# Moving the scale and shift of a normed operand to GpSimd, and re-staging a mixer's input projection

## The chip, the cores and the metric

The kernel runs on one core of a Trainium2 chip. The metric is the device time of one execution in microseconds (us). The core's engines work side by side and wait for one another by semaphores: TensorE (PE, matrix products), VectorE (DVE), ScalarE (ACT), GpSimd (POOL) and SyncE (SP, which issues the transfers). Each runs its own list of instructions in the order in which the program wrote them.

## The reference, cut to what matters

A diffusion backbone of two layers works on 384 tokens: 256 latent ones and 128 of context. Each layer is a feed-forward stage, a mixer and another feed-forward stage, all in fp32.

```python
h = rmsnorm(x, g_norm[l, 0]) * (1.0 + sc1) + sh1
x = x + 0.5 * gt1 * swiglu(h, ffn1_w13[l], ffn1_w2[l])
h = rmsnorm(x, g_norm[l, 1]) * (1.0 + sc2) + sh2
m, k_state, v_state = mixer(h, l, ctx_kv, use_rope)
x = x + gt2 * m
h = rmsnorm(x, g_norm[l, 2]) * (1.0 + sc3) + sh3
x = x + 0.5 * gt3 * swiglu(h, ffn2_w13[l], ffn2_w2[l])
...
# in the mixer
proj = h @ w_in[l]
z, q, k, v, gates = split(proj)
u, zv = split(gelu(z))
a = u * (w_spatial @ rmsnorm(zv, sgu_gain) + b_spatial)      # gating unit, in chunks of 128 tokens
b = differential attention of q, k, v                        # 8 heads, rotary on the latent tokens
m = (sigmoid(g_a) * (a @ w_branch_a) + sigmoid(g_b) * (b @ w_branch_b)) @ w_out
```

`sc`, `sh` and `gt` come from a modulation product of the conditioning vectors, one set for the context tokens and one for the latent ones.

## The kernel before, in words

**Three products for one.** TensorE multiplies in a rounded fp32 format, so every operand is held as two parts: `hi` (a rounded copy, made by ScalarE, L406 for activations and L180 for weights) and `lo` (the rest, a subtraction on VectorE, L409 and L183). Each product is the sum of hi x hi, lo x hi and hi x lo (`mm3`, L232 to L234; L386 to L388 in token-major form). Weights come in chunks of 128 x 1024 (`raw`), loaded by SP ahead of time and split into `whi` and `wlo`, four buffers each, by `split_upto`; the `lo` halves are deferred by a few steps.

**Jobs.** The program is a list of jobs, written out in the order in which TensorE is to do them. A column job (`col_job`) makes one 128 x 384 tile of a result in eight k-steps of three matmuls. A token-major job set (`tokmajor_job`) makes three accumulators of 128 x 512 in four jobs; its operands are swapped, so that tokens lie on the partitions. Both take PSUM buffers `mm` from a ring of four. After its matmuls a job's `evac` is written; the next job follows. Other work is written between jobs: `bg`, a list of functions of which `run_bg` pops one (or two while more than six are left) at the start of each job with a weight chunk, and `mods.put()`, which writes one step of the modulation product (mostly two VectorE passes over a 128 x 1024 chunk, L437; at a piece's end two reductions, L443).

**The lead of a stage.** While the norm of x is not yet known, products start on the operand `u` = x times the scale (unnormed, with the shift in two extra columns, so 386 wide), and the evacuation applies the norm: `normed` copies the two shift columns (L607) and multiplies the PSUM tile by the broadcast norm `rb` (L608), both on VectorE, and ScalarE then applies the function with the shift as bias (L725 in the mixer, L645 in the feed-forward). `lead` takes the first columns this way: three as a group, the others as column jobs. Beside the latter, `make_h` makes the operand `h` proper, eight tiles: POOL multiplies x by `rb` (L564), ScalarE applies scale and shift in two pieces, for the latent and the context tokens (L573), and the tile is split (L406, L409). The tiles pass through `t`, five buffers that the evacuations use as well. A feed-forward stage has eight such columns, the mixer six. Five of the six stages have a lead; the first stage of layer 0 starts in another way.

**The mixer's order.** The lead makes six of the eight tiles of `u` in the reference's sense (tile `m["u"]`, columns u0 to u5). Then come two token-major sets for `zv` (`zv_evac`, L735, L736), with a modulation step after each job; then `push_sgu` puts the gating unit into `bg` (the norm `sgu_norm`; the scales of the token groups 0 and 1; the scale of group 2 with block 0; blocks 1 to 7). Columns u6, u7 (with a modulation step after each), q and k of head 0, and two token-major sets for v follow, then attention with the rest of the columns woven in. A block is six matmul instructions on TensorE (L764) and then VectorE (L768, L771) and a split; its PSUM tile `tp` has one buffer. `zv` and `v` share a slot (`spare("Z", 1)`), so the first v evacuation flushes `bg`. The k evacuation copies k on ScalarE and turns it by the rotary on VectorE (L784 to L787).

Of the kernel before, what the change touches and what calls it, by code (L numbers as in the profile page):

```python
# [11 lines left out]
AF = mybir.ActivationFunctionType  # L12
ALU = mybir.AluOpType
AX = mybir.AxisListType

P = 128
D = 1024
# [16 lines left out]
SH1, SC1, GT1, SH2, SC2, GT2, SH3, SC3, GT3 = range(9)  # L34
TOK = ((1, 0, 256), (0, 256, 384))
# [5 lines left out]
def hybrid_step(  # L41
# [5 lines left out]
    T, V, S, G = nc.tensor, nc.vector, nc.scalar, nc.gpsimd  # L47
# [29 lines left out]
    modT = cp.tile([P, DEPTH, 9, KD, 2], F32, name="modT")  # L77
    amod = cp.tile([P, 3, KD, 2], F32, name="amod")

    x = cp.tile([P, KD, NT], F32, name="x")  # L80
# [84 lines left out]
    def run_later(n=1):  # L165

        for e in later:
            e[0] -= n
        while later and later[0][0] <= 0:
            later.pop(0)[1]()  # L170
# [25 lines left out]
    bg = []  # L196

    def run_bg(n=1):
        for _ in range(n):
            if bg:  # L200
                bg.pop(0)()

    def step():
        while True:
            if st["cur"] is None:
                if st["job"] >= len(jobs):
                    return False
                j = jobs[st["job"]]
                st["job"] += 1
                st["cur"] = j.gen(j.first)  # L210
                if j.n:
                    run_bg(2 if len(bg) > 6 else 1)
            try:
                next(st["cur"])
                run_later()
                return True
            except StopIteration:
                st["cur"] = None
# [17 lines left out]
    def col_job(key, rhs, evac, n=NT, beside=()):  # L236

        def gen(c):
            hi, lo = w_get(c)
            ps = ps_mm()  # L240
            r_hi, r_lo = rhs()
            for kt in range(KD):
                sl = slice(kt * P, (kt + 1) * P)
                mm3(ps[:, :n], hi[:, sl], lo[:, sl], r_hi[:, kt, :], r_lo[:, kt, :], kt == 0, kt == KD - 1)
                for at, f in beside:
                    if at == kt:
                        f()
                yield
            evac(ps[:, :n])
        Job([key], gen)  # L250
# [27 lines left out]
    def lead(keys, evacs, l, i, pc_sh):  # L278
        lead_group(keys[:3], evacs[:3], l, i)
        make = make_h(l, i, pc_sh)  # L280
        n = len(keys) - 3
        at = [divmod(e * (KD * n - 6) // KD + 2, KD) for e in range(KD)]
        for e in range(n):
            beside = [(kt, lambda k=k: make(k)) for k, (j, kt) in enumerate(at) if j == e]
            col_job(keys[3 + e], rhs_u, evacs[3 + e], NU, beside)
# [84 lines left out]
    def tokmajor_job(keys, lhs, evac, mods=None):  # L370
        state = {}

        def mk(i):
            def gen(c):
                hi, lo = w_get(c)
                if i == 0:
                    state["ps"] = [ps_mm() for _ in range(3)]
                l_hi, l_lo = lhs()
                for k2 in range(2):
                    kt = 2 * i + k2  # L380
                    sl = slice(k2 * 512, (k2 + 1) * 512)
                    for j in range(3):
                        ts_ = slice(j * P, (j + 1) * P)
                        ps = state["ps"][j]
                        first, last = kt == 0, kt == KD - 1
                        T.matmul(ps, lhsT=l_hi[:, kt, ts_], rhs=hi[:, sl], start=first, stop=False)  # L386
                        T.matmul(ps, lhsT=l_hi[:, kt, ts_], rhs=lo[:, sl], start=False, stop=False)  # L387
                        T.matmul(ps, lhsT=l_lo[:, kt, ts_], rhs=hi[:, sl], start=False, stop=last)  # L388
                        if j == 0:
                            yield  # L390
                        elif j == 1:
                            yield
                        else:
                            yield
                            yield
                if i == 3:
                    for j in range(3):
                        evac(j, state["ps"][j])
            return gen
        for i in range(4):  # L400
            Job([keys[i]], mk(i))
            if mods:
                mods.put()
# [88 lines left out]
    nst = {}  # L492
# [65 lines left out]
    def make_h(l, i, pc_sh):  # L558
        xr = {}

        def scaled(kt):
            if kt < KD:
                xr[kt] = tmp()
                G.tensor_tensor(out=xr[kt], in0=x[:, kt, :], in1=nst["rb"], op=ALU.mult)  # L564

        def make(kt):
            if kt == 0:
                nst["h"] = duo(role["Y"])
                scaled(0)
            scaled(kt + 1)  # L570
            t = xr.pop(kt)
            for n, s0, s1 in TOK:
                S.activation(  # L573
                    out=t[:, s0:s1], in_=t[:, s0:s1], func=AF.Identity, scale=amod[:, i, kt, n:n + 1],
                    bias=modT[:, l, pc_sh, kt, n:n + 1])
            split_act(nst["h"][0][:, kt, :], nst["h"][1][:, kt, :], t)
        return make

# [129 lines left out]
    def mixer(l, mods, after):  # L708
        lam_init = 0.8 - 0.6 * math.exp(-0.3 * l)
        m = {}  # L710

        def spare(p, n, shape):
            return slot(2 * role[p] + n, shape)

        def u_evac(f, u):
            def e(ps):
                if "u" not in m:
                    m["u"] = spare("Z", 0, [P, KD, NT])
                t = m["u"][:, f, :]
                if not u:  # L720
                    S.activation(out=t, in_=ps, func=AF.Gelu_apprx_tanh)
                    return
                b = normed(ps, t)
                for n, s0, s1 in TOK:
                    S.activation(  # L725
                        out=t[:, s0:s1], in_=t[:, s0:s1], func=AF.Gelu_apprx_tanh, bias=b[:, n:n + 1])
            return e

        def zv_evac(hf):
            def e(j, ps):  # L730
                if "zv" not in m:
                    m["zv"] = spare("Z", 1, [P, 3, D])
                    m["ssq"] = tiny(6, "ys")
                z = m["zv"][:, j, hf * 512:(hf + 1) * 512]
                S.activation(out=z, in_=ps, func=AF.Gelu_apprx_tanh)  # L735
                S.activation(out=ps, in_=z, func=AF.Square, accum_out=m["ssq"][:, 2 * j + hf:2 * j + hf + 1])  # L736
            return e
# [37 lines left out]
        def flush_bg():  # L775
            while bg:
                run_bg(1)
            run_later(99)
# [30 lines left out]
        def v_evac(hf):  # L809
            def e(j, ps):  # L810
                if "v" not in m:
                    m["v"] = spare("Z", 1, [P, 3, D])
                sl = slice(hf * 512, (hf + 1) * 512)
                if j == 1:
                    V.tensor_copy(out=m["v"][:, j, sl], in_=ps)
                else:
                    S.activation(out=m["v"][:, j, sl], in_=ps, func=AF.Copy)
                if j == 2:
                    nc.sync.dma_start(out=a["new_v"][l][:, sl], in_=m["v"][:, 2, sl])
            return e  # L820
# [37 lines left out]
        def wk(pair, half):  # L858
            return ("w_in", l, pair, half)

        Job([], lambda c: iter_once(lambda: (turn(), sgu_prep())))
        lead([wk(f // 2, f % 2) for f in range(6)], [u_evac(f, True) for f in range(6)], l, 1, SH2)

        def push_sgu():
            bg.append(sgu_norm)
# [5 lines left out]
        tokmajor_job([wk(4, 0), wk(4, 1), wk(5, 0), wk(5, 1)], rhs_h, zv_evac(0), mods)  # L871
        tokmajor_job([wk(6, 0), wk(6, 1), wk(7, 0), wk(7, 1)], rhs_h, zv_evac(1), mods)
        Job([], lambda c: iter_once(push_sgu))
        for f in range(6, 8):
            col_job(wk(f // 2, f % 2), rhs_h, u_evac(f, False))
            mods.put()
        col_job(wk(8, 0), rhs_h, q_evac(0))
        col_job(wk(8, 1), rhs_h, k_evac(0))

        vk = [wk(16 + i // 2, i % 2) for i in range(8)]  # L880
        tokmajor_job(vk[:4], rhs_h, lambda j, ps: (flush_bg() if j == 0 else None, v_evac(0)(j, ps)))
        tokmajor_job(vk[4:], rhs_h, v_evac(1))
        att_start = len(jobs)

# [6 lines left out]
        while side or hq < NH:  # L891
# [7 lines left out]
            else:  # L899
                kind, f = side.pop(0)  # L900
# [177 lines left out]
    with tc.manual_schedule():  # L1078
# [7 lines left out]
        for q in range(3):  # L1086
            for n in range(2):
                t = slot(2 * role["ZWX"[q]] + n, [P, 2048])
# [6 lines left out]
        for e in range(4):  # L1095
            V.tensor_copy(
                out=tiled[32 * e:32 * e + 32, :].rearrange("p (a b) -> p a b", a=4),
                in_=ident[32 * e:32 * e + 32, 32 * e:32 * e + 32].unsqueeze(1).to_broadcast([32, 4, 32]))
# [8 lines left out]
        while step():  # L1107
            pass
# [5 lines left out]
        for dt in range(KD):  # L1114
            V.scalar_tensor_tensor(
                out=y[:, dt, :], in0=x[:, dt, :], scalar=gfin[:, dt:dt + 1], in1=nst["rb"],
                op0=ALU.mult, op1=ALU.mult)
# [80 lines left out]
```

## Time and profile before

| | us |
|---|---|
| median of 3 runs | 1976.28 (1975.49 to 1976.9) |
| profiled execution | 1981.81 |
| its span, first to last instruction | 1980.0 |
| TensorE busy in it | 1927.4 |
| VectorE busy | 1325.1 |
| ScalarE busy | 835.1 |
| GpSimd busy | 175.6 |
| mean granted TensorE clock | 0.986 |

The profile lists what each engine did in one execution. In a timeline, a row gives the start and length in us, the engine, the line of the code, the operation, output and inputs, and in brackets how long the engine had been idle and what ended that. Since matmuls overlap, starts tell more than lengths there. In a list of waits a row gives who waited for whom, the total in us, the times and the longest. A group row gives the busy time in us, the mean in ns and the idle time ahead of it. Columns that are made in a row on TensorE take 4.2 us each.

### The profile page before, as it was taken

To read this page: it belongs to the slowest core of one execution; us is meant where nothing else is said; L and a number is where in the kernel's file an instruction comes from. 1 tells how busy PE (TensorE), PEld (TensorE's weight loads), DVE (VectorE), ACT (ScalarE), POOL (GpSimd) and SP (SyncE) were. 2 spreads that over 40 slices of the span, in tenths; PEclk is the share of its full clock that TensorE was granted. 3 is DMA by queue.
4 is the path that set the end of the run, shared out by engine and by line. 5 is a ranking of instruction groups with operands and counts; after the bars stand their busy time and mean duration, and the time that the engine had idled before them with its cause. 6 is when DMAs were issued, how large, how long until landed. Compare 5 with 4: busy or idle time off the path is not lost.

```text
span 1980.0 us, 28463 instructions
## 1 busy us (share of the span) xinstructions
PE 1927.4 (97%) x10902; PEld 1850.9 (93%) x10902; DVE 1325.1 (67%) x2014; ACT 835.1 (42%) x1515; POOL 175.6 (9%) x447
## 2 busy tenths in 40 slices
PE   6999999899999999999999999998999999999997
PEld 5999998789889999999999999987889999999997
DVE  5777874757666767778758779567576546655533
ACT  4433335436653355333353333363456534533321
POOL 0000001003431010000010000010143300100000
PEclk9999999899999999999999999998999999999998
DMA  8665663543334535667536656444423333354430
GB/s 321 197 198 193 211 201 107 192 131 101 101 104 156 164 108 189 195 196 226 169 100 213 199 192 224 161 145 136 132 98 98 107 125 121 97 180 157 143 116 33
DMA packets 92152, 308.69 MB, mean 156 GB/s; under 512 B 10864, under 2 KB 18416, under 8 KB 91248
## 3 DMA queue, kind: packets, MB, share of 16 engines
q1 hardware_dynamic: 91584, 306.76, 47.7%
q8 instruction: 86, 1.41, 0.3%
q14 instruction: 50, 0.41, 0.1%
q10 hardware_dynamic: 432, 0.11, 0.0%
HBM read 303.16 MB, written 3.67 MB: 155 GB/s over the span
## 4 chain that ended last, share of the span: by engine, by line
PE 78%; issue 14%; ACT 4%; DVE 3%; DMA 1%; POOL 0%; DVEq 0%; POOLq 0%; SPq 0%; ACTq 0%
PE mm L232 22%; PE mm L233 22%; PE mm L234 22%; PE mm L386 2%; PE mm L388 2%; PE mm L387 2%; PE sc L938 2%; ACT t L573 1%; PE mm L987 1%; ACT whi L180 1%; ACT S L406 1%; PE tp L764 1%; PE tp L971 1%; DMA raw<-in_ffn_w 1%; DVE wlo L183 0%
## 5 line engine op out<-in xcount | busy, mean ns | idle before, releaser
L232 PE MATMUL mm<-S,whi 128*128 128x384 f32 (+1 forms) x3136 | 1078.2, 344 | 6.7 <-ACT S L406 4.8
L233 PE MATMUL mm<-S,wlo 128*128 128x384 f32 (+1 forms) x3136 | 1061.5, 338 | 0.0
L234 PE MATMUL mm<-S,whi 128*128 128x384 f32 (+1 forms) x3136 | 1059.9, 338 | 0.2
L183 DVE TENSOR_TENSOR wlo<-raw,whi 128x1024 fp32r<-128x1024 f32 x424 | 521.0, 1229 | 256.7 <-ACT whi L180 255.1
L232 PEld LDWEIGHTS mm<-S,whi 128*128 128x128 f32 x3136 | 592.1, 189 | 31.1 <-issue 19.1
L234 PEld LDWEIGHTS mm<-S,whi 128*128 128x128 f32 x3136 | 591.3, 189 | 2.4 <-DVE S L409 2.2
L233 PEld LDWEIGHTS mm<-S,wlo 128*128 128x128 f32 x3136 | 592.0, 189 | 0.3
L180 ACT ACTIVATE whi<-raw 128x1024 fp32r<-128x1024 f32 x424 | 445.1, 1051 | 215.9 <-PE mm L234 118.0
L437 DVE SCALAR_TENSOR_TENSOR acc<-raw,scond,acc 128x1024 f32<-128x1024 f32 x224 | 277.2, 1278 | 0.0
L406 ACT ACTIVATE S<-t 128x384 fp32r<-128x384 f32 x144 | 75.6, 525 | 320.8 <-DVE t L660 244.4
L507 POOL TENSOR_TENSOR yr<-yv,nhalf 128x3 f32<-128x3 f32 x9 | 7.7, 857 | 1380.6 <-DVE yv L524 1289.5
L409 DVE TENSOR_TENSOR S<-t,S 128x384 fp32r<-128x384 f32 x144 | 84.2, 585 | 51.3 <-ACT S L406 51.0
L660 DVE TENSOR_TENSOR t<-t,mm 128x384 f32<-128x384 f32 x76 | 42.1, 554 | 80.4 <-PE mm L234 80.4
L641 ACT ACTIVATE t<-mm 128x384 f32<-128x384 f32 x76 | 37.2, 490 | 139.0 <-PE mm L234 139.0
L386 PE MATMUL mm<-whi,S 128*128 128x512 f32 x192 | 78.2, 407 | 8.3 <-DVE S L608 8.3
L388 PE MATMUL mm<-whi,S 128*128 128x512 f32 x192 | 77.4, 403 | 0.0
L387 PE MATMUL mm<-wlo,S 128*128 128x512 f32 x192 | 76.9, 400 | 0.0
L500 ACT ACTIVATE t<-x 128x384 f32<-128x384 f32 x49 | 25.0, 522 | 110.0 <-DVE x L616 110.0
L616 DVE SCALAR_TENSOR_TENSOR x<-mm,modT,x 128x256 f32<-128x256 f32 x96 | 35.6, 412 | 34.7 <-PE mm L234 34.2
L386 PEld LDWEIGHTS mm<-whi,S 128*128 128x128 f32 x192 | 37.0, 193 | 17.7 <-issue 9.1
L950 ACT ACTIVATE e<-sc,ym 128x384 f32<-128x384 f32 (+1 forms) x96 | 47.9, 507 | 6.6 <-DVE ym L941 6.2
L564 POOL TENSOR_TENSOR t<-x,rb 128x384 f32<-128x384 f32 x40 | 43.0, 1086 | 83.0 <-DVE S L409 52.9
(133 smaller groups left out, 1168.3 us busy)
## 6 DMA issues: line engine op xcount, KB each, us to landing
raw<-in_ffn_w SPq DMA_DIRECT2D x264, 512.0 KB, 4.3
raw<-in_w_mod SPq DMA_DIRECT2D x132, 512.0 KB, 4.6
raw<-in_w_in SPq DMA_DIRECT2D x112, 512.0 KB, 3.8
raw<-in_w_branch_a SPq DMA_DIRECT2D x16, 512.0 KB, 3.6
raw<-in_w_branch_b SPq DMA_DIRECT2D x16, 512.0 KB, 3.6
raw<-in_w_out SPq DMA_DIRECT2D x16, 512.0 KB, 3.7
S<-in_w_mod SPq DMA_DIRECT2D x6, 1024.0 KB, 9.2
x<-in_x SPq DMA_DIRECT2D x4, 384.0 KB, 4.1
```

The costliest lines, as they stand in the source:

```text
L180: S.activation(out=hi, in_=raw, func=AF.Copy)
L183: V.tensor_tensor(out=lo, in0=raw, in1=hi.bitcast(F32), op=ALU.subtract)
L232: T.matmul(ps, lhsT=w_hi, rhs=r_hi, start=first, stop=False)
L233: T.matmul(ps, lhsT=w_lo, rhs=r_hi, start=False, stop=False)
L234: T.matmul(ps, lhsT=w_hi, rhs=r_lo, start=False, stop=last)
L386: T.matmul(ps, lhsT=l_hi[:, kt, ts_], rhs=hi[:, sl], start=first, stop=False)
L387: T.matmul(ps, lhsT=l_hi[:, kt, ts_], rhs=lo[:, sl], start=False, stop=False)
L388: T.matmul(ps, lhsT=l_lo[:, kt, ts_], rhs=hi[:, sl], start=False, stop=last)
L406: S.activation(out=dst_hi, in_=src, func=AF.Copy)
L409: V.tensor_tensor(out=dst_lo, in0=src, in1=dst_hi.bitcast(F32), op=ALU.subtract)
L437: V.scalar_tensor_tensor(out=acc[n], in0=raw, scalar=s, in1=acc[n], op0=ALU.mult, op1=ALU.add)
L950: S.activation(out=e[:, i, 0:nk], in_=sc[:, i, 0:nk], func=AF.Exp, scale=0.125, bias=mx[:, i:i + 1], accum_out=z[:, i:i + 1])
```

## The change

The scale and shift of `make_h` move from ScalarE to POOL, right behind the product with `rb`. The mixer's lead takes all eight columns of u, so u6 and u7 no longer come after `push_sgu`. The token-major values `zv` get a slot of their own, the one that held the u operand, and the first v evacuation does not flush. `run_bg` pops one function a job. The two modulation steps that followed u6 and u7 become four, behind the jobs of the first v set; fewer are left for later in the mixer of layer 0.

```diff
-                    run_bg(2 if len(bg) > 6 else 1)
+                    run_bg(1)
...
         def scaled(kt):
             if kt < KD:
                 xr[kt] = tmp()
-                G.tensor_tensor(out=xr[kt], in0=x[:, kt, :], in1=nst["rb"], op=ALU.mult)
+                t = xr[kt]
+                G.tensor_tensor(out=t, in0=x[:, kt, :], in1=nst["rb"], op=ALU.mult)
+                for n, s0, s1 in TOK:
+                    G.tensor_scalar(
+                        out=t[:, s0:s1], in0=t[:, s0:s1], scalar1=amod[:, i, kt, n:n + 1],
+                        scalar2=modT[:, l, pc_sh, kt, n:n + 1], op0=ALU.mult, op1=ALU.add)
...
             t = xr.pop(kt)
-            for n, s0, s1 in TOK:
-                S.activation(
-                    out=t[:, s0:s1], in_=t[:, s0:s1], func=AF.Identity, scale=amod[:, i, kt, n:n + 1],
-                    bias=modT[:, l, pc_sh, kt, n:n + 1])
             split_act(nst["h"][0][:, kt, :], nst["h"][1][:, kt, :], t)
...
-                    m["zv"] = spare("Z", 1, [P, 3, D])
+                    m["zv"] = spare("X", 0, [P, 3, D])
...
-        lead([wk(f // 2, f % 2) for f in range(6)], [u_evac(f, True) for f in range(6)], l, 1, SH2)
+        lead([wk(f // 2, f % 2) for f in range(8)], [u_evac(f) for f in range(8)], l, 1, SH2)
...
-        for f in range(6, 8):
-            col_job(wk(f // 2, f % 2), rhs_h, u_evac(f, False))
-            mods.put()
         col_job(wk(8, 0), rhs_h, q_evac(0))
         col_job(wk(8, 1), rhs_h, k_evac(0))
...
-        tokmajor_job(vk[:4], rhs_h, lambda j, ps: (flush_bg() if j == 0 else None, v_evac(0)(j, ps)))
+        tokmajor_job(vk[:4], rhs_h, v_evac(0), mods)
```

How it moves instructions, first on ScalarE, in the mixer's lead of layer 0 (S_2888 is the result u, S_2947 the hi part of h). Before, from the evacuation of u2 to the weight split behind u3's:

```order
L725 ACTIVATE S_2888<-S_2888,yb 128x256
L725 ACTIVATE S_2888<-S_2888,yb 128x128
L180 ACTIVATE whi<-raw 128x1024
L573 ACTIVATE t<-t,modT,amod 128x256
L573 ACTIVATE t<-t,modT,amod 128x128
L406 ACTIVATE S_2947<-t 128x384
```

and now, where L723 is the old L725:

```order
L723 ACTIVATE S_2888<-S_2888,yb 128x256
L723 ACTIVATE S_2888<-S_2888,yb 128x128
L180 ACTIVATE whi<-raw 128x1024
L406 ACTIVATE S_2947<-t 128x384 x2
L723 ACTIVATE S_2888<-S_2888,yb 128x256
```

The pairs L573 are gone, and two tiles of h are made per column where there were three or four.

On POOL in the same place, before (eight products in a row):

```order
L507 TENSOR_TENSOR yr<-yv,nhalf 128x3 x2
L564 TENSOR_TENSOR t<-x,rb 128x384 x8
L507 TENSOR_TENSOR yr<-yv,nhalf 128x3
L508 TENSOR_TENSOR ye<-yv,yr 128x3
L510 TENSOR_TENSOR ye<-ye,yr 128x3
```

and now, the first two tiles:

```order
L507 TENSOR_TENSOR yr<-yv,nhalf 128x3 x2
L565 TENSOR_TENSOR t<-x,rb 128x384
L567 TENSOR_SCALAR t<-t,amod,modT 128x256
L567 TENSOR_SCALAR t<-t,amod,modT 128x128
L565 TENSOR_TENSOR t<-x,rb 128x384
```

Each product is followed by its two pieces of scale and shift.

On VectorE at the start of the gating unit of layer 0 (S_3205 and S_3277 are zv), before:

```order
L748 TENSOR_TENSOR yv<-ys 128x3
L749 TENSOR_SCALAR yv<-yv 128x3
L753 TENSOR_SCALAR S_3205<-S_3205,yr 128x1024 x2
L183 TENSOR_TENSOR wlo<-raw,whi 128x1024
L443 TENSOR_REDUCE red<-acc 128x32 x2
L753 TENSOR_SCALAR S_3205<-S_3205,yr 128x1024
L768 SCALAR_TENSOR_TENSOR t<-tp,sgain,bb 128x384
```

and now, from the rotary of q on:

```order
L785 TENSOR_TENSOR qf<-qf,t 128x256
L751 TENSOR_SCALAR S_3277<-S_3277,yr 128x1024 x2
L183 TENSOR_TENSOR wlo<-raw,whi 128x1024
L782 STREAM_SHUFFLE t<-kf 128x256
L783 TENSOR_TENSOR t<-t,sin_t 128x256
L784 TENSOR_TENSOR kf<-kf,cos_t 128x256
L785 TENSOR_TENSOR kf<-kf,t 128x256
L751 TENSOR_SCALAR S_3277<-S_3277,yr 128x1024
L766 SCALAR_TENSOR_TENSOR t<-tp,sgain,bb 128x384
```

The scale of group 2, which stood behind two reductions of the modulation, stands behind the rotary of k.

More of the change, by code (lines that the diff above doesn't have):

```diff
@@ L713, in spare, with u_evac @@
             return slot(2 * role[p] + n, shape)
-        def u_evac(f, u):
+        def u_evac(f):
             def e(ps):
@@ L719, in e @@
                 t = m["u"][:, f, :]
-                if not u:
-                    S.activation(out=t, in_=ps, func=AF.Gelu_apprx_tanh)
-                    return
                 b = normed(ps, t)
```

## The prediction

> **What bounds the kernel now.** I read the page first, then what TensorE waited for, then the timelines of TensorE, VectorE, ScalarE and GpSimd around the longest waits.
>
> ```profile
> PE 1927.4 (97%) x10902; PEld 1850.9 (93%) x10902; DVE 1325.1 (67%) x2014; ACT 835.1 (42%) x1515; POOL 175.6 (9%) x447
> PE tp L764 <- DVE S L753: 10.6, 6, 3.6
> PE mm L386 <- DVE S L608: 8.3, 2, 4.1
> PE mm L232 <- ACT S L406: 4.8, 6, 1.3
> ```
>
> TensorE is the bound: 97% busy, so only its waits and its slow stretches can be won. The three lines below the first are what it waits for inside the layers: the gating unit's first blocks (L764), the third accumulator of the first token-major job (L386), and the first h column of a feed-forward stage (L232). Each leaves more behind than the wait.
>
> ```profile
> 337.17 0.40 PE L386 MATMUL mm<-whi,S 128*128 128x512 f32 x1
> 342.87 0.47 PE L386 MATMUL mm<-whi,S 128*128 128x512 f32 x1 [4.14 <-DVE S L608]
> 347.98 0.39 PE L386 MATMUL mm<-whi,S 128*128 128x512 f32 x1
> ...
> 376.82 0.34 PE L232 MATMUL mm<-S,whi 128*128 128x384 f32 x1
> 382.74 0.49 PE L764 MATMUL tp<-ws,S 128*128 128x128 f32 x2 [1.55 <-DVE S L753]
> 387.45 0.80 PE L764 MATMUL tp<-ws,S 128*128 128x128 f32 x2 [3.56 <-DVE S L753]
> ...
> 396.92 0.89 PE L764 MATMUL tp<-ws,S 128*128 128x128 f32 x6
> ...
> 1033.06 0.34 PE L232 MATMUL mm<-S,whi 128*128 128x384 f32 x1
> 1035.01 0.44 PE L232 MATMUL mm<-S,whi 128*128 128x384 f32 x1 [1.26 <-ACT S L406]
> 1040.91 0.33 PE L232 MATMUL mm<-S,whi 128*128 128x384 f32 x1
> ```
>
> In TensorE's timeline a k-step of a column (three matmuls) takes 0.525 us undisturbed, a step of 512 columns 0.70.
> A, token-major start: from 337.17 to 347.98 lie 7 steps, 4.9 us of work in 10.81: 5.9 lost, 4.1 of it waiting, 1.8 at a slower pace after it. In the other mixer I count 6.5 the same way. Together 12.4.
> B, gating unit: from 376.82 to 396.92 lie two columns (8.4) and two blocks (0.65 each in later rows), 9.7 us of work in 20.1: 10.2 lost; the other mixer likewise. Together 20.4.
> D, feed-forward start: from 1033.06 to 1040.91 lie 7 steps, 3.7 us in 7.85: 4.1 lost; the other two stages lose 4.1 and 2.7. Together 10.9.
>
> **The change, part by part.** Eight tiles on u instead of six: the columns u6 and u7 move ahead of the token-major jobs, with 2 more of 386 elements per matmul: 2x2 columns x 4.2 us x 0.5%, below 0.1 us. Their weight loads move with them on SP's queue; nothing in the chain of waits is a weight load there. The two columns also give two more VectorE scalings (L608), which A's walk contains.
>
> *The gating unit (B).* The one-step pop and the moved columns put the norm into the q column, scales 0 and 1 into the k column, and scale 2 with block 0 at the first v job. Behind the k column VectorE now holds, in program order, the rotary of k and then scale 2, and block 0's third product waits for them.
>
> ```profile
> 381.23 0.49 ACT L721 ACTIVATE S<-mm 128x384 f32<-128x384 f32 x1 [0.82 <-PE mm L234]
> 408.11 0.44 DVE L784 STREAM_SHUFFLE t<-kf 128x256 f32<-128x256 f32 x1
> 409.38 0.42 DVE L787 TENSOR_TENSOR kf<-kf,t 128x256 f32<-128x256 f32 x1
> 384.40 2.36 DVE L443 TRANSPOSE_TENSOR_REDUCE red<-acc 128x32 f32<-128x1024 f32 x2
> 386.69 0.71 DVE L753 TENSOR_SCALAR S<-S,yr 128x1024 f32<-128x1024 f32 x1
> 413.60 0.61 DVE L768 SCALAR_TENSOR_TENSOR t<-tp,sgain,bb 128x384 f32<-128x384 f32 x1
> 417.49 0.61 DVE L768 SCALAR_TENSOR_TENSOR t<-tp,sgain,bb 128x384 f32<-128x384 f32 x1
> ```
>
> ScalarE's copy ends 0.7 us after the column's last matmul (column end 381.03, copy 381.23 to 381.72), the rotary takes 1.7 (408.11 to 409.80), scale 2 takes 0.71: 3.1 us after the k column, less 0.45 for the two products that can run, so 2.7 of stall once per mixer, plus a slow stretch that I take as A's 1.8: 4.5. Scales 0 and 1 (1.4 us) are hidden by the k column, and the two reductions L443, which stood ahead of scale 2 and were 2.36 of the 3.56 us, go behind the first v job. There a block's VectorE loop takes 3.9 us (413.60 to 417.49) of the 4.9 that job and block take on TensorE; four modulation steps of about L443's 2.4 us each, less 1.0 spare, put VectorE up to 6 us behind, which the four v jobs without them win back, and a block there needs only the one before it. B falls from 20.4 to 9.0: 11.4 saved. Ends: 7 (a stall of 5 us each) and 20 (no stall).
> The token-major values get slot X0, whose last reader is the u operand, done before; so v needs no flush, and nothing is paid.
>
> *Scale and shift on POOL (A and D).* 80 ScalarE operations go, 80 POOL operations come, and each pair stands between the product L564 and the split.
>
> ```profile
> L564 POOL TENSOR_TENSOR t<-x,rb 128x384 f32<-128x384 f32 x40 | 43.0, 1086 | 83.0 <-DVE S L409 52.9 <-ACT rb L538 20.5 <-DVE t L656 8.1
> L508 POOL TENSOR_TENSOR ye<-y,yr 128x1 f32<-128x1 f32 x48 | 11.4, 238 | 3.8
> L993 POOL TENSOR_SCALAR y<-y 128x1 f32<-128x1 f32 x48 | 14.8, 308 | 4.2
> L511 POOL TENSOR_SCALAR ye<-ye 128x1 f32<-128x1 f32 x48 | 9.6, 200 | 4.2
> ```
>
> No wide POOL tensor_scalar is in the trace. L564 against L508 gives about 2.15 ns an element with two tensor inputs. Upper end: 0.31 fixed and that slope, 0.86 and 0.58. Lower end: 0.20 fixed and half the slope, 0.47 and 0.34. I take 0.85 for the pair, near the lower end, since it reads one tensor. A tile then costs POOL some 2 us, eight 16 us; the lead lasts 25 us after rb, so POOL's own time is covered. What isn't is what it does to VectorE:
>
> ```profile
> 727.49 1.22 DVE L183 TENSOR_TENSOR wlo<-raw,whi 128x1024 fp32r<-128x1024 f32 x1
> 727.66 1.94 POOL L564 TENSOR_TENSOR t<-x,rb 128x384 f32<-128x384 f32 x1 [2.68 <-DVE t L656]
> 728.63 1.38 DVE L409 TENSOR_TENSOR S<-t,S 128x384 fp32r<-128x384 f32 x1
> ```
>
> POOL's product waits until the VectorE operation is over, and then the next VectorE operation (0.56 alone) waits for the product: operations of two SBUF inputs take turns with POOL. A VectorE operation with one of its inputs in PSUM (L608) shows no such lengthening in the trace. The loop that sets the leads is this one:
>
> ```profile
> 342.10 0.15 DVE L607 COPY yb<-mm 128x2 f32<-128x2 f32 x1
> 343.46 1.04 ACT L180 ACTIVATE whi<-raw 128x1024 fp32r<-128x1024 f32 x1
> 344.41 0.97 ACT L573 ACTIVATE t<-t,modT,amod 128x256 f32<-128x256 f32 x2
> 344.54 1.23 DVE L183 TENSOR_TENSOR wlo<-raw,whi 128x1024 fp32r<-128x1024 f32 x1 [1.82 <-ACT whi L180]
> 346.04 0.56 DVE L409 TENSOR_TENSOR S<-t,S 128x384 fp32r<-128x384 f32 x1 [0.28 <-ACT S L406]
> 346.51 0.15 DVE L607 COPY yb<-mm 128x2 f32<-128x2 f32 x1
> ```
>
> One evacuation (L607) to the next, with one tile h in between: 4.4 us. Without the pair, VectorE's own wlo is the later one (it ends 345.77) and two splits follow, 1.03: a loop of 4.7 us with two tiles, against 4.2 us of matmuls. So even without POOL's turns each column falls 0.5 behind. Its three two-input operations each meet a POOL operation: half the mean of 1.02, 0.48 and 0.37, weighted by length, is 0.37 us; I take 0.35 in the mixer, where POOL has the tiles in hand, and 0.24 in the feed-forward, where it waits for buffers for a third of the time.
> Mixer, counted from rb at 320.0:
>
> ```profile
> 320.04 4.92 POOL L564 TENSOR_TENSOR t<-x,rb 128x384 f32<-128x384 f32 x5 [4.04 <-ACT rb L538]
> 328.39 1.23 DVE L183 TENSOR_TENSOR wlo<-raw,whi 128x1024 fp32r<-128x1024 f32 x1 [0.69 <-ACT whi L180]
> ```
>
> u3 is evacuated at 9.6 + 1.03 = 10.65, and u6, whose bank the third accumulator takes, at 10.65 + 3x4.7 + 0.6 = 25.4 without turns, and 25.4 + 9x0.35 = 28.5 with them. It is wanted two columns later than before, 337.17 + 8.4 + 0.5 = 26.0 after rb. Stall 2.5 and a slow stretch of 1.8, 4.3 per mixer instead of 5.9 and 6.5: A saves 3.7. Ends: 12.4 (no turns), and a loss of 8 (each of nine operations waiting 1.02).
> Feed-forward, third stage:
>
> ```profile
> 1704.02 0.15 DVE L607 COPY yb<-mm 128x2 f32<-128x2 f32 x1
> 1710.96 0.15 DVE L607 COPY yb<-mm 128x2 f32<-128x2 f32 x1
> 1716.88 0.15 DVE L607 COPY yb<-mm 128x2 f32<-128x2 f32 x1
> 1721.31 0.56 DVE L409 TENSOR_TENSOR S<-t,S 128x384 fp32r<-128x384 f32 x1 [0.27 <-ACT S L406]
> ```
>
> From the third evacuation to the split of tile 6, which the first h column waits for, the loops take 5.9 + 6.9 + 5.9 + 5.0 = 23.8. Without the pairs and turns they would be 4.7 + 5.5 + 4.7 + 4.7 = 19.6; 17 two-input operations x 0.24 put back 4.1. The split comes where it came: D saves 0.1 a stage, 0.3. Ends: 10.9, and a loss of 39 at 1.02 a turn.
> Sum: 11.4 + 3.7 + 0.3 - 0.1 = 15.3 us. The profiled execution took 1981.8 (span 1980.0), so it would take 1966.5; the median shown is 5.5 lower, 1976.3 to 1961.
>
> **The rivals.** *The turns cost nothing* (a one-input POOL operation need not take VectorE's reads; only the two-input product is seen to): A and D vanish, 12.4 + 10.9 + 11.4 - 0.1 = 34.6, 1942. For it: ScalarE, which ended each loop, loses four pairs of 0.97, 3.9 us, in every two columns of 8.4. *The gating unit gives nothing*: VectorE comes into the q and k columns late, block 0 waits as long as before, 1961 + 11 = 1972; against it, the norm's end is two columns off. *Slower*: POOL's tensor_scalar is dearer than its product. The working above is 33.9 - 18.5s with s the turns relative to mine; it is nil at s = 1.8 and a loss over 4 from 2.05, where a turn averages 0.75 us. Operations of 2 and 1 us give that (half the weighted mean of 1.02, 2 and 1), and POOL's eight tiles then take 33 us, past the lead's 25, which costs the leads some 3 us more: 1985. The upper end above, 1.44 for a pair, is well short of it.
> *Short stalls leave no slow stretch.* At 1035 the trace has 4.1 us lost for some 1.6 of waiting (the 4.8 us of the waits row over three stages), so I count 1.8 behind each new stall; without the four, 7.2 less: 1954. The Trainium skill, TensorE: Matmul & The Clock Gate, Part 1, says the clock falls after an idle window of about 3.4 us; by that rule the new stalls of 2.5 and 2.7 us would leave none, and the trace disagrees.
>
> **How the numbers follow.** My walk 0.52 (1953 to 1969), no turns 0.20, no slow stretch 0.05, gating unit without gain 0.13, slower 0.10. The range takes in no turns and gating unit: 1940 to 1974. A change within 0.2%, 4 us, can hardly be told from none: faster 0.82 (the first three and some of the fourth), same 0.08, slower 0.10.
>
> **What would show it.** Right: one wait of about 2.7 us per mixer before the third product of the first block, none at its other blocks; VectorE's wlo and splits in the leads at 1.3 to 2 us and 0.6 to 1.4 while POOL is busy nearly throughout; a wait of 2 to 3 us at the third token-major accumulator; the first h column waiting 1 to 2 us. Wrong: no waits at the leads' ends (the turns are cheap), POOL tensor_scalars over 1 us, or waits at blocks 1 to 7.

## The result, and the profile after

| | before | after |
|---|---|---|
| median, us | 1976.59 (1975.49 to 1977.11) | 1945.41 (1944.28 to 1946.55) |
| profiled execution | 1981.81 | 1946.55 |
| its span | 1980.0 | 1944.7 |
| TensorE busy | 1927.4 | 1912.1 |
| ScalarE busy | 835.1 | 797.7 |
| GpSimd busy | 175.6 | 249.6 |
| mean granted clock | 0.986 | 0.994 |

The change makes the kernel 31.2 us faster: a ratio of 0.9843, 95% interval 0.9826 to 0.986. The forecast was 1961 in a range of 1940 to 1974, so the time lies in the range, but the saving is twice the one worked out (15.6). The time lies there only because the range took in the rival without turns, which had said 1942.

What TensorE waited for in the kernel after, inside the layers (total, times, longest in us; L550 is the first stage's start, the same in both kernels):

```profile
PE tp L762 <- DVE S L751: 5.1, 2, 2.5
PE mm L232 <- ACT S L550: 2.0, 2, 1.7
```

Of the three groups of waits one is left, that of the gating unit (L762 is the old L764), once per mixer. TensorE's timeline at the three places, layer 0:

```profile
345.60 0.40 PE L386 MATMUL mm<-whi,S 128*128 128x512 f32 x1
346.29 0.40 PE L386 MATMUL mm<-whi,S 128*128 128x512 f32 x1
346.98 0.39 PE L386 MATMUL mm<-whi,S 128*128 128x512 f32 x1
347.68 0.39 PE L386 MATMUL mm<-whi,S 128*128 128x512 f32 x1
...
387.74 0.61 PE L762 MATMUL tp<-ws,S 128*128 128x128 f32 x4
390.88 0.49 PE L762 MATMUL tp<-ws,S 128*128 128x128 f32 x2 [2.53 <-DVE S L751]
391.12 0.48 PE L386 MATMUL mm<-whi,S 128*128 128x512 f32 x1
395.55 0.40 PE L386 MATMUL mm<-whi,S 128*128 128x512 f32 x1
```

The first rows are the three token-major accumulators and the next step: 0.69 us apart, no wait; A's 12.4 us are gone whole. In the rows from 387.74 on the wait is 2.53 us, and the four steps from 391.12 to 395.55 take 4.43 us in place of 2.8. From 387.74, a block (0.65) and four steps would have ended at 391.2: 4.35 us are lost in this mixer, and 4.1 in the other, counted the same way. The prediction put the loss before at 10.2 a mixer; its own rows, 20.1 less 9.7, give 10.4, and 10.3 in the other mixer. So B gains 20.7 - 8.4 = 12.3. The first h columns of the feed-forward stages show no wait at all. Added up: 12.4 + 12.3 + 10.9 = 35.6, against 35.3 us between the spans. The medians differ by 4 us less: the profiled execution of the kernel before was 5.2 us above its median, and since other executions of it have 1981.0 us at a granted clock of 0.987 and 1976.2 at 0.989, its slow stretches probably differ in length from one to the next.

### The profile page after: what moved, and what is told of

It reads as the page before. It is cut to its first block, busy times and chain, and to the rows that moved or that the text cites. A ratio compares the mean times of both kernels' runs of the same rounds, so it can differ in the third digit from the quotient of the medians.

```text
span 1944.7 us, 28452 instructions
## 1 busy us (share of the span) xinstructions
PE 1912.1 (98%) x10902; PEld 1841.9 (95%) x10902; DVE 1327.9 (68%) x2022; ACT 797.7 (41%) x1439; POOL 249.6 (13%) x527
## 4 chain that ended last, share of the span: by engine, by line
PE 84%; issue 13%; DVE 1%; POOL 1%; DMA 1%; ACT 0%; SPq 0%; POOLq 0%; DVEq 0%; ACTq 0%
PE mm L232 24%; PE mm L233 24%; PE mm L234 24%; PE mm L386 2%; PE mm L388 2%; PE mm L387 2%; PE sc L932 2%; PE mm L981 1%; PE tp L965 1%; PE tp L762 1%; DMA raw<-in_ffn_w 1%; POOL t L567 0%; PE sc L301 0%; POOL t L565 0%; PE ms L1004 0%
## 5 line engine op out<-in xcount | busy, mean ns | idle before, releaser
L232 PE MATMUL mm<-S,whi 128*128 128x384 f32 (+1 forms) x3136 | 1073.8, 342 | 2.0 <-ACT S L550 2.0
L232 PEld LDWEIGHTS mm<-S,whi 128*128 128x128 f32 x3136 | 589.5, 188 | 24.6 <-issue 19.1
L567 POOL TENSOR_SCALAR t<-t,amod,modT 128x256 f32<-128x256 f32 x80 | 66.7, 842 | 4.2
L617 DVE SCALAR_TENSOR_TENSOR x<-mm,modT,x 128x256 f32<-128x256 f32 x96 | 35.6, 413 | 34.6 <-PE mm L234 34.2
L565 POOL TENSOR_TENSOR t<-x,rb 128x384 f32<-128x384 f32 x40 | 49.8, 1245 | 29.0 <-ACT rb L538 20.4
```

Source lines behind the costliest of these rows:

```text
L232: T.matmul(ps, lhsT=w_hi, rhs=r_hi, start=first, stop=False)
L567: G.tensor_scalar(out=t[:, s0:s1], in0=t[:, s0:s1], scalar1=amod[:, i, kt, n:n + 1], scalar2=modT[:, l, pc_sh, kt, n:n + 1], op0=ALU.mult, ...
```

## The experiments

**Each half alone.** The kernel before with scale and shift on POOL, all else as before:

```diff
-                G.tensor_tensor(out=xr[kt], in0=x[:, kt, :], in1=nst["rb"], op=ALU.mult)
+                t = xr[kt]
+                G.tensor_tensor(out=t, in0=x[:, kt, :], in1=nst["rb"], op=ALU.mult)
+                for n, s0, s1 in TOK:
+                    G.tensor_scalar(out=t[:, s0:s1], ...)
...
-            for n, s0, s1 in TOK:
-                S.activation(out=t[:, s0:s1], in_=t[:, s0:s1], func=AF.Identity, ...)
```

> The kernel before with one part of the change alone: scale and shift on POOL, the mixer's lead still of six columns, gating unit and slots as before. Theory P (each tile of h now costs POOL about 3.1 us under VectorE's load, as in the changed kernel, where eight took 24.8 us, and VectorE hardly waits): the three feed-forward leads are long enough, their 10.9 us vanish; the mixer's lead of six columns is not (about 17 us after the norm against 25 of POOL), so the third token-major accumulator waits at least as long as before, 4 to 7 us; gating unit unchanged. 1976.6 - 10.9 + 0 to 6 = 1966 to 1972. Rival S (the feed-forward's gain needs something else of the change as well): 1974 to 1978. Rival M (POOL's part alone also frees the mixer's lead): 1976.6 - 10.9 - 12.4 = 1953.

And the changed kernel with the same edit taken back, so that only the eight columns, the slot and the order of the gating unit stay:

> The changed kernel with scale and shift back on ScalarE: eight columns on u, own slot, one pop and the new place of the modulation steps stay. Theory P: the feed-forward leads lose their 10.9 us again; the gating unit keeps its gain of 11.7; in the mixer the loop from one evacuation to the next is ScalarE's again (5.9 us with two tiles), u6 is evacuated about 30 us after the norm where 26 is wanted, so about 4 us of wait and 2 of slow stretch per mixer come back: 1976.6 - 11.7 = 1965, 1960 to 1968. Rival C (two more columns cover the operand whatever engine makes it): the mixer keeps its 12.4: 1976.6 - 11.7 - 12.4 = 1952.5.

POOL alone: 1965.78 us, ratio 0.9939 (0.9923 to 0.9955), 10.9 less than the 1976.72 of before. Order alone: 1966.05, ratio 0.9942 (0.9923 to 0.9961), 10.7 less. TensorE's waits, POOL alone first, then order alone:

```profile
PE tp L765 <- DVE S L754: 10.6, 6, 3.6
PE mm L386 <- DVE S L609: 6.6, 2, 3.4
```

```profile
PE mm L386 <- DVE S L608: 6.2, 2, 3.1
PE tp L761 <- DVE S L750: 5.1, 2, 2.5
PE mm L232 <- ACT S L406: 4.7, 6, 1.3
```

POOL alone clears the feed-forward's wait (no row L232 from ScalarE is left there) and leaves the gating unit; order alone does the opposite. The token-major wait stands in both, 3.4 and 3.1 us at the longest instead of 4.1. Counted over seven steps as in the prediction, the two mixers together still lose 8.6 us there with POOL alone and 9.1 with order alone, of the 12.4 before. Only the whole change clears it: 31.2 us against 10.9 + 10.7 = 21.6, so 9.6 us belong to neither half (some 6 either way, by the three intervals). With six columns POOL's eight tiles come too late: ahead of the evacuation that the third accumulator waits for, ScalarE's last three splits each wait 1.6 to 1.7 us for POOL. With eight columns and ScalarE's pairs in the loop, a column's evacuation follows the last by 5.9 us, and TensorE takes 4.2. Theory P's account fits both, though POOL alone came out a little below its range and its wait below the 4 to 7 us; rivals S, M and C fell. Which edit of the order gives the gating unit its gain (eight columns, one pop, the slot or the moved modulation steps) was not separated.

**The wait that is left.** The third scale goes into the pop of the first two, ahead of k's rotary:

```diff
-            bg.append(lambda: (sgu_scale(0), sgu_scale(1)))
-            bg.append(lambda: (sgu_scale(2), sgu_block(0)()))
+            bg.append(lambda: (sgu_scale(0), sgu_scale(1), sgu_scale(2)))
+            bg.append(sgu_block(0))
```

> The changed kernel with the third scale moved into the pop of the first two, ahead of the rotary of k, so that block 0 finds it done. Theory: the 2.5 us wait before the third product of block 0 and the slow stretch behind it go, 4.35 us per mixer by the changed kernel's trace: 1945.4 - 8.7 = 1937, 1935 to 1940. Rival: the rotary of k and the next weight split come 0.7 us later, block 0's second products or the first attention unit wait instead: 1941 to 1945.

1939.17 us, ratio 0.9805 (0.979 to 0.982): 6.2 us under the changed kernel's median, at the slow end of what was expected. The wait at block 0 is gone, and small ones have come:

```profile
PE mm L386 <- ACT S L815: 0.9, 1, 0.9
PE tp L762 <- DVE t L766: 0.5, 1, 0.5
```

Both lie in layer 0 at the end of the first v set. There VectorE, with the modulation steps among the blocks, is late with a block, ScalarE waits for it with a split, and ScalarE's evacuation of v (L815) stands behind that. So the cause of the 2.5 us is shown: scale 2 behind the rotary.

**POOL's work in the leads, made longer.** Two versions of the changed kernel, with more work per tile: a second pair of one-input pieces, or a second product with two inputs. Both were meant to take about 1 us.

```diff
+                for n, s0, s1 in TOK:
+                    G.tensor_scalar(out=t[:, s0:s1], in0=t[:, s0:s1], scalar1=1.0, scalar2=0.0, op0=ALU.mult, op1=ALU.add)
```

> The changed kernel with a second pair of tensor_scalar pieces on POOL for each tile of h (times 1, plus 0, in place): POOL's work for a tile goes from 2.1 to 3.1 us alone. Theory V (one-input POOL operations give way to VectorE and hardly hold it up, two-input ones take turns with it): VectorE's weight splits and splits of h keep their lengths in the leads; POOL's tiles come late, eight in 33 us or more where the leads have 25; waits come back at the leads' ends, 3 to 8 us each with slow stretches: 1960 to 1985. Theory T (all POOL operations take turns with VectorE alike): the same lateness, and VectorE's two-input operations are lengthened as much as in the run with an extra product. Rival H (POOL has time to spare): 1945 to 1949.

```diff
+                t3 = t.rearrange("p (j q) -> p j q", j=3)
+                G.tensor_tensor(out=t3, in0=t3, in1=ones.unsqueeze(1).to_broadcast([P, 3, P]), op=ALU.mult)
```

> The changed kernel with an extra product on POOL for each tile of h (times a tile of ones, two inputs, 1.0 us alone, as long as the extra pair in the other run). Theory V: VectorE's splits of h and of weights in the leads are lengthened clearly more than with the extra pair (splits of h above 0.65 us in the mean, where the changed kernel has 0.59), and the time is 3 to 15 us above that of the extra pair. Theory T: time and lengths as with the extra pair, within 2 us.

Extra pair: 1972.21 us, ratio 0.9958 (0.9944 to 0.9972). Extra product: 1985.9, ratio 1.0034 (1.0022 to 1.0045), slower than before the change. So POOL has no time to spare (rival H fell). Between the two lie 13.7 us. The groups of VectorE and POOL and the waits, extra pair first:

```profile
L183 DVE TENSOR_TENSOR wlo<-raw,whi 128x1024 fp32r<-128x1024 f32 x424 | 520.3, 1228 | 248.7 <-ACT whi L180 247.9
L660 DVE SCALAR_TENSOR_TENSOR t<-t,yb 128x128 f32<-128x128 f32 x12 | 5.6, 469 | 0.0
PE mm L386 <- DVE S L612: 8.8, 2, 4.5
PE mm L232 <- ACT S L406: 3.4, 4, 1.1
```

```profile
L183 DVE TENSOR_TENSOR wlo<-raw,whi 128x1024 fp32r<-128x1024 f32 x424 | 527.4, 1245 | 247.4 <-ACT whi L180 246.1 <-DMA bb<-in_b_spatial 0.4
L660 DVE SCALAR_TENSOR_TENSOR t<-t,yb 128x128 f32<-128x128 f32 x12 | 8.6, 719 | 0.0
PE mm L386 <- DVE S L612: 14.6, 4, 6.5
PE mm L232 <- ACT S L406: 12.3, 6, 2.9
```

With the extra product the weight splits take 7.1 us more in all, and the pieces L660 (the old L656) 719 ns instead of 469. The splits of h, for which over 0.65 us was expected, were not lengthened (0.587 in the mean): that part missed. Nor does the extra pair take 1 us: with its scalars written into the instruction (immediates) it takes 0.67 alone, against 1.00 for the pair with scalars from tiles and 1.02 for the product. So a part of the 13.7 us is plain length, and this test does not settle how much of it comes from what the operation reads.

**The turns by themselves.** In the changed kernel, ten POOL operations whose output is not used run against VectorE's dense work in the second token-major set, one-input in layer 0, two-input in layer 1:

```diff
+                if hf == 0 and j == 2:
+                    z0, z1 = m["zv"][:, 0, 0:NT], m["zv"][:, 1, 0:NT]
+                    pj = tmp()
+                    for _ in range(10):
+                        if l == 0:
+                            G.tensor_scalar(out=pj, in0=z0, scalar1=1.0, scalar2=0.5, op0=ALU.mult, op1=ALU.add)
+                        else:
+                            G.tensor_tensor(out=pj, in0=z0, in1=z1, op=ALU.mult)
```

> The changed kernel with ten unneeded POOL operations of 128x384 each mixer, during the second token-major set, where VectorE is busy for some 90% with two-input operations (weight splits 1.22 us, modulation passes 1.24): in layer 0 tensor_scalar with immediates, in layer 1 a product of two SBUF tiles; their output is not used. Theory V: in layer 0 VectorE's operations keep 1.22 to 1.28 us and POOL's are stretched, in part to over 2 us; in layer 1 most of VectorE's operations that meet a product are lengthened by 0.3 to 1 us, up to 8 us in all. Theory T: both layers alike. Time within 2 us of the changed kernel's in layer 0's case, some us more if layer 1's VectorE falls behind.

One execution: 1950.41 us, 5 us above the changed kernel's median; the gating unit waits 9.4 us in it in place of 5.1. POOL and VectorE in layer 0, then in layer 1; the first VectorE row of each stands ahead of POOL's operations:

```profile
360.63 14.40 POOL L740 TENSOR_SCALAR t<-S 128x384 f32<-128x384 f32 x10 [17.02 <-ACT S L733]
357.81 2.48 DVE L437 SCALAR_TENSOR_TENSOR acc<-raw,scond,acc 128x1024 f32<-128x1024 f32 x2
368.80 1.52 DVE L183 TENSOR_TENSOR wlo<-raw,whi 128x1024 fp32r<-128x1024 f32 x1
370.24 2.97 DVE L437 SCALAR_TENSOR_TENSOR acc<-raw,scond,acc 128x1024 f32<-128x1024 f32 x2
...
1312.04 19.40 POOL L742 TENSOR_TENSOR t<-S 128x384 f32<-128x384 f32 x10 [18.12 <-ACT S L733]
1306.99 1.21 DVE L183 TENSOR_TENSOR wlo<-raw,whi 128x1024 fp32r<-128x1024 f32 x1
1320.68 2.04 DVE L183 TENSOR_TENSOR wlo<-raw,whi 128x1024 fp32r<-128x1024 f32 x1
1322.64 3.99 DVE L437 SCALAR_TENSOR_TENSOR acc<-raw,scond,acc 128x1024 f32<-128x1024 f32 x2
```

Neither theory holds as stated. Both kinds take turns with VectorE, about one operation for one: ten POOL operations need 14.4 and 19.4 us, and VectorE does some ten in that time. But a turn costs VectorE 0.30 us (1.52 against 1.22) or 0.25 (2.97 against 2.48, for two) behind a one-input operation, and 0.82 or 0.75 behind a product, three times as much.

**Fewer steps among the blocks.** The kernel with the early scale, without the modulation steps in the first v set:

```diff
-        tokmajor_job(vk[:4], rhs_h, v_evac(0), mods)
+        tokmajor_job(vk[:4], rhs_h, v_evac(0))
```

> The kernel with the third scale moved ahead, and without the modulation steps behind the first v set: they are made in attention's gate columns, as far as they were not already, and layer 0 has just enough places for them there. Theory: VectorE is no longer behind at the end of the first v set of layer 0, ScalarE's evacuation there is in time, and the 0.95 us wait with its slow stretch, some 3 us in layer 0, goes: 1939.2 - 3 = 1936, 1934 to 1938. Rival: the gate columns have no room and lose as much: 1938 to 1942.

1937.43 us, ratio 0.9786 (0.9769 to 0.9802). The two small waits are gone, and attention's columns show none in their place. Against the early scale alone (0.9805, 0.979 to 0.982) the intervals overlap, so a gain over it is not shown; the kernel is faster than both kernels of the change.

## Why the prediction was half right

**Gating unit: right.** The forecast was 2.7 us of wait and 4.5 lost per mixer; the trace has 2.53 of wait, and 4.35 and 4.1 lost. The term of 11.4 measured 12.3 by the traces; with the slip in the loss before put right, the forecast would have been 11.8. Order alone, which also shortens the token-major wait, brings 10.7 by medians. The place was right too: the early scale takes the wait away. No wait came at blocks 1 to 7, so the modulation steps stay covered.

**Slow stretch: right for these stalls, but not for every wait.** Behind the 2.53 us of waiting the next four steps took 1.6 us more in layer 0 and 1.2 in layer 1. The granted clock from 391.12 to 395.55 is 0.61, and 1.00 in the steps after it. So the rival without slow stretches does not describe this trace. Nor does the rule in TensorE: Matmul & The Clock Gate (Part 1) of the Trainium skill, by which the clock falls after an idle window of about 3.4 us: 2.53 us was enough. But the size of the term, 1.8 us behind each stall, does not hold everywhere. With POOL alone two waits of nearly the same length end like this, in layer 0 and in layer 1:

```profile
340.69 0.48 PE L386 MATMUL mm<-whi,S 128*128 128x512 f32 x1 [3.36 <-DVE S L609]
341.74 0.63 PE L386 MATMUL mm<-whi,S 128*128 128x512 f32 x1
343.02 0.63 PE L386 MATMUL mm<-whi,S 128*128 128x512 f32 x1
...
1301.82 0.47 PE L386 MATMUL mm<-whi,S 128*128 128x512 f32 x1 [3.29 <-DVE S L609]
1302.59 0.40 PE L386 MATMUL mm<-whi,S 128*128 128x512 f32 x1
1303.28 0.39 PE L386 MATMUL mm<-whi,S 128*128 128x512 f32 x1
```

The first is followed by steps of up to 1.28 us at a granted clock of 0.61, the second by steps of 0.69 at 1.00. What decides between the two is not shown.

**The turns: the step that failed.** I let each two-input VectorE operation wait 0.35 us in the mixer and 0.24 in the feed-forward, as half the weighted length of POOL's operations. That price was too high, and it was put on VectorE alone, where POOL pays more. In the mixer of the kernel after, u3 is evacuated at 329.88, and u6 leaves its bank in the last two rows:

```profile
329.88 0.15 DVE L608 COPY yb<-mm 128x2 f32<-128x2 f32 x1
332.31 1.68 DVE L183 TENSOR_TENSOR wlo<-raw,whi 128x1024 fp32r<-128x1024 f32 x1 [1.82 <-ACT whi L180]
339.74 0.81 DVE L409 TENSOR_TENSOR S<-t,S 128x384 fp32r<-128x384 f32 x1 [0.75 <-ACT S L406]
344.87 0.53 ACT L406 ACTIVATE S<-t 128x384 fp32r<-128x384 f32 x1 [1.59 <-POOL t L567]
345.43 0.56 DVE L409 TENSOR_TENSOR S<-t,S 128x384 fp32r<-128x384 f32 x1 [0.83 <-ACT S L406]
345.91 0.15 DVE L608 COPY yb<-mm 128x2 f32<-128x2 f32 x1
345.98 0.55 DVE L609 TENSOR_TENSOR S<-mm,rb 128x384 f32<-128x384 f32 x1
```

That is 26.5 us after rb (320.0), where the working gave 25.4 without turns and 28.5 with them. Part of this is luck: u3 came at 9.9 after rb and not at 10.65. The three loops from u3 to u6 took 16.0 us, where the working had 14.1 without turns and 17.2 with them. Of their nine two-input operations, two were lengthened, by 0.7 us in all (1.68 in place of 1.23, and 0.81 in place of 0.55): 0.08 each, not 0.35. The rest of the delay came in another way: in the last two loops VectorE waited 0.75 and 0.83 us for ScalarE's split, and ScalarE for a tile that POOL had not finished. In the second feed-forward stage of layer 0:

```profile
718.30 0.15 DVE L608 COPY yb<-mm 128x2 f32<-128x2 f32 x1
738.80 1.02 DVE L409 TENSOR_TENSOR S<-t,S 128x384 fp32r<-128x384 f32 x2
```

The first of the two splits in the last row is that of tile 6; with 0.56 for its length it ends 21.1 us after the third evacuation, where the working had 19.6 without turns and 23.7 with them: 0.09 an operation, not 0.24. The probe shows one reason: a POOL operation stands in VectorE's way for 0.25 to 0.30 us if it has one input, and even a product of 1.02 for no more than 0.82. The rest POOL pays, and that was left out of the sum:

```profile
L565 POOL TENSOR_TENSOR t<-x,rb 128x384 f32<-128x384 f32 x40 | 49.8, 1245 | 29.0 <-ACT rb L538 20.4 <-DVE S L409 6.8 <-DVE t L657 1.8
L567 POOL TENSOR_SCALAR t<-t,amod,modT 128x256 f32<-128x256 f32 x40 | 34.6, 864 | 4.2
L567 POOL TENSOR_SCALAR t<-t,amod,modT 128x128 f32<-128x128 f32 x40 | 32.8, 820 | 0.0
311.00:346.00 35.00, 35.00 (x203) 34.90 (x202) 19.98 (x41) 17.91 (x32) 24.83 (x25) 1.00 0.37 120
```

The pair, 0.85 in the forecast, takes 1.00 alone (by the timeline) and 1.68 in the mean of the leads. The last row is the window of layer 0's mixer lead: POOL is busy for 24.83 of its 35 us, almost all of it with the eight tiles, 3 us each where I had some 2.

**When the bank is wanted: a slip.** I set the third accumulator 0.5 us after the start of the token-major job. The rows at 345.60 and 346.98 put it at 1.4, so 27.0 us after rb and not 26.0. With that, u6's 26.5 is in time by less than 0.5 us; with my turns it would have been 1.5 late. A's term was 3.7 and measured 12.4, D's 0.3 and measured 10.9; both ends, 12.4 and 10.9, stood in the text, as the rival to which I gave 0.20. Its sum of 34.6 is near the 35.3 of the spans, though turns are not free, as the probe shows: they were short enough for both waits to vanish.

**Slower by a dear tensor_scalar.** That did not come, but the margin is thin: 1.02 us more of two-input POOL work per tile puts the kernel above its old time.

## What to carry to other kernels

An operand's making can leave a loaded engine for an idle one at a lower price than the length of the moved operations suggests, if what moves reads one tensor. Take the price of a turn from a row where the two engines really meet, and charge it to both of them. Two edits that each give a part can free a wait that neither frees alone, so work out the wait with all of them in place, and count to the matmul that really needs the buffer. When work pops out of a queue at job starts, look at what the engine already holds from the job before: scale 2 behind a rotary cost 6 us that one line gives back.

## What the runs showed of the hardware

In the probe VectorE and POOL alternated, about one operation for one, while VectorE worked on two-input operations from SBUF: products of 128x384, 1.02 us alone, came every 1.94 us, and the weight splits between them took 2.04 instead of 1.22. With one-input operations on POOL the splits took 1.52. A tensor_scalar with both scalars from tiles costs POOL 1.00 us for the pieces of 256 and 128, with immediates 0.67. Waits of 2.53 and 3.36 us were followed by steps of up to 1.28 us in place of 0.70, at a granted clock of 0.61; one of 3.29 us was not.
